# Attention's PSUM tiles: two banks for the scores of both maps, a head's output and norm together, one bank for transposes

## The chip, the cores and the metric

The kernel runs on one core of a Trainium2 chip. The metric is the device time of one execution in microseconds (us). Engines are named as in the profile: PE is the matmul engine (TensorE), PEld its weight loads, DVE VectorE, ACT ScalarE, POOL GpSimd, SP the engine that issues the transfers. PSUM is the memory that PE writes, and DVE and ACT read: eight banks, each of 128 partitions by 512 float32 here.

## What is computed

One layer of a bidirectional encoder, for 512 positions of 1024 channels in float32: a modulated RMS norm, three token mixers side by side (differential attention, HGRN2, GLA), their outputs merged through sigmoid gates, an output projection, then a squared-ReLU MLP and a last norm. The change touches differential attention alone, which has 4 heads. Each head has two maps of 64 query and key channels, and values of 128 channels:

```python
scores = jnp.einsum('bhiqd,bhikd->bhiqk', qb, k).astype(jnp.float32) * scale
scores = scores - slopes[:, None, None, None] * dist
p = jax.nn.softmax(scores, axis=-1)
w = p[:, :, 0] - lam * p[:, :, 1]
return jnp.einsum('bhqk,bhkv->bhqv', w.astype(v.dtype), v)
...
o = rms_norm(o, subln_g) * (1.0 - lam_init)
```

Positions are swept in query blocks of 128, so a head has four of them.

## The kernel before

A float32 product is made of three matmuls: each operand is split into a high part and a low part (suffixes h and l), and hi x hi, lo x hi and hi x lo are summed in one PSUM bank. All wide projections are made so, by `mm3` (L220 to L222): for a gate such as gb5 there are 8 slices of 128 input channels (h0 to h7) and so 24 matmuls of 512 columns. A weight is loaded raw, cast to its high part on ACT (L215) and subtracted to its low part on DVE (L216).

PSUM has three pools: `pm` with three banks (wide projections, gates, merges), `pl` with three (`ps_lv`) and `pt` with two (`ps_ms`). In attention, `pl` holds scores and `pt` the transposes, a head's output and the sum of its norm.

For each head and query tile, `attention(hd)` (L795 to L829) issues: six score matmuls, three for each of the two maps. Map 0 sits on partitions 0 to 63 and map 1 on 64 to 127, so each uses half of the array's rows (L807); a DVE operation for each map that adds the position penalty and takes the row maximum (L811), an exponential on ACT (L814), the sums' reciprocals and the weighted difference of the maps on DVE (L817 to L820), four transposes on PE (L823) and four copies on ACT (L825). After the four query tiles come the head's output `oa` (L828, four float32 matmuls) and `head_norm`: Square on ACT (L643), a matmul with ones that sums over partitions (L645), Ln and Exp on ACT (L177, L178, with a table load each), the scaling on DVE (L647, out An0sq to An3sq), and the split into An0oh and An0ol (L184, L185). These are inputs to `upa0` to `upa7` in the loop behind attention, next to the gates `ga0` to `ga7` (`proj_a`).

Between these pieces of attention the kernel has PE work that does not depend on it: a queue of generators (`pump`, `later`, `need`) holds the merge of the other two mixers, `merge_bc(m)`, with the gates `gb` and `gc` and the products `up`. `merge_bc` also loads modulation tiles of 512 KB (`ada16` to `ada47`, four of them for each m) and reduces each on DVE (`ada_tile`, L164). They share four buffers with the raw weights. The order of instructions on each engine is not that of the code: it is set when the kernel is built, by a scheduler that replays the program against its own model of durations and takes whichever instruction is ready; buffers of a pool bound what is ready. On the chip each engine runs its instructions strictly in that order, and an instruction waits by semaphore for the others that it needs.

Of the kernel before, what the change touches and what calls it, by code (L numbers as in the profile page):

```python
# [11 lines left out]
F32 = mybir.dt.float32  # L12
# [5 lines left out]
PSUM = bass.MemoryType.PSUM  # L18

P = 128  # L20
S = 512
# [33 lines left out]
def tile_trunk(ctx, tc, xT, cols, lam_p, w2blk, ada, slab, wtok, wlr, wck, wcq, wg, watt, wgate, wup_bc, wup_a, wout,  # L55
# [4 lines left out]
    def pool_of(name, n, side="left"):  # L60
        return tc.tile_pool(name=name, bufs=n, side=side, reuse_waits="tile")
# [15 lines left out]
    sm = ms_.enter_context(pool_of("sm", 4))  # L77
    sm.tile([P, 8], F32, tag="fill", name="smfill")
    pm = ctx.enter_context(tc.tile_pool(name="pm", bufs=3, space=PSUM))
    pl = ctx.enter_context(tc.tile_pool(name="pl", bufs=3, space=PSUM))  # L80

    def st(name, dt=F32, pool=None):
        return (pool or gp).tile([P, S], dt, tag="t", name=name)
# [4 lines left out]
    def ps_lv(name):  # L88
        return pl.tile([P, S], F32, tag="lv", name=name)

    def ps_ms(name):
        return pt.tile([P, S], F32, tag="ms", name=name)
# [21 lines left out]
    ones128 = c2.tile([P, P], F32, name="ones128")  # L114
# [60 lines left out]
    def rstd_of(ms, name, pool):  # L175
        L = st(name + "l", pool=pool)
        A.activation(L, ms, AF.Ln, bias=eps[:, 0:1])  # L177
        A.activation(L, L, AF.Exp, scale=-0.5)  # L178
        return L

    def split(src, name, pool):

        hi, lo = (pool.tile([P, S], F32R, tag="t", name=name + e) for e in "hl")
        A.copy(hi, src)  # L184
        V.tensor_tensor(lo, src, hi.bitcast(F32), ALU.subtract)  # L185
        return hi, lo
# [8 lines left out]
    def pump(n):  # L195

        while queue and n > 0:
            try:
                next(queue[0])
                n -= 1  # L200
            except StopIteration:
                queue.popleft()
# [67 lines left out]
    with tc.tile_pool(name="ad0", bufs=8, side="right", reuse_waits="tile") as ad0, \  # L270
# [59 lines left out]
        for k in range(KT):  # L330
# [12 lines left out]
            f = t  # L343
# [20 lines left out]
                for u in us:  # L364
                    mm3(slab_ps[u], wh[:, u * P:(u + 1) * P], wl[:, u * P:(u + 1) * P], hi, lo, False, k == KT - 1)
        lb, neglam, gsub, gb40, masks, bm, w2b, nd = small_operands()
    pt = ctx.enter_context(tc.tile_pool(name="pt", bufs=2, space=PSUM))

    def proj(src, name):
        wh, wl = weights(src, name, [P, KT, P])  # L370
# [267 lines left out]
                                  masks[:, li - 2, :].unsqueeze(1).to_broadcast([P, 8, 64]),  # L638
                                  ps.rearrange("p (n t) -> p n t", n=8))

    def head_norm(o, n, blk, g, extra, pool, dst):
        sq = st(n + "sq", pool=pool)
        A.activation(sq, o, AF.Square)  # L643
        ms = ps_ms(n + "ms")
        T.matmul(ms, blk, sq, start=True, stop=True)  # L645
        rs = rstd_of(ms, n + "rs", pool)
        V.scalar_tensor_tensor(sq, o, g, rs, ALU.mult, ALU.mult)  # L647
        if extra is not None:
            V.scalar_tensor_tensor(sq, sq, 0.5, extra, ALU.mult, ALU.mult)
        return split(sq, n + "o", dst)  # L650
# [69 lines left out]
    for j in range(2):  # L720
        npump = NP[j]
        def done(pr, o, j=j):
            if j == 0:
                need(f_bg[1])
                silu_of(0)
                silu_of(1)
            obc[j] = head_norm(o, f"Hn{j}", blk64, C("g_hg"), sg[j], cp[j], op)
        scan_tile(f"H{j}", cp[j], gp, gp, *hg[j], (0, 64), 0, (j,), f_bi, npump, done)
# [4 lines left out]
    def gdone(pr, o):  # L733
        need(f_gate)
        if pr == 0:
            tables_of_logs(last_tanh[0])
        obc[2 + pr] = head_norm(o, f"Gn{pr}", blk64, C("g_gl"), sg[2 + pr], cp[0], op)
# [46 lines left out]
    zs.close()  # L784
    ys.close()
    zs, ys = ExitStack(), ExitStack()
    oap = zs.enter_context(pool_of("oap", 8))
    fp = ys.enter_context(pool_of("fp", 8, "right"))
    es = ExitStack()
    ep = es.enter_context(pool_of("ep", 12, "right"))  # L790
    wtp = es.enter_context(pool_of("wtp", 4, "right"))
    part = []
    oa = []

    def attention(hd):  # L795
        slope = 2.0 ** (-2 * (hd + 1))
        qh, ql, kh, kl = qk[hd]
        wT = [st(f"wT{hd}{k}", pool=wtp) for k in range(4)]
        for qt in range(4):
            qs = slice(qt * P, (qt + 1) * P)  # L800
            e = []
            mx = sm.tile([P, 8], F32, tag="mx", name=f"mx{hd}{qt}")
            sc = [ps_lv(f"s{hd}{qt}{i}") for i in range(2)]
            for n_, (q_, k_) in enumerate(((qh, kh), (qh, kl), (ql, kh))):
                for i in range(2):
                    rr = slice(64 * i, 64 * i + 64)
                    T.matmul(sc[i], q_[rr, qs], k_[rr, :], start=n_ == 0, stop=n_ == 2)  # L807
            pump(NA)
            for i in range(2):
                s_ = st(f"e{hd}{qt}{i}", pool=ep)  # L810
                V.tensor_tensor_reduce(s_, sc[i], nd[:, 384 - P * qt:896 - P * qt], scale=slope, scalar=-3e38,  # L811
                                       op0=ALU.add, op1=ALU.max, accum_out=mx[:, i:i + 1])
                V.tensor_scalar(mx[:, 2 + i:3 + i], mx[:, i:i + 1], -1.0, None, ALU.mult)  # L813
                A.activation(s_, s_, AF.Exp, bias=mx[:, 2 + i:3 + i], accum_out=mx[:, 4 + i:5 + i])  # L814
                e.append(s_)
            pump(NA)
            V.reciprocal(mx[:, 6:8], mx[:, 4:6])  # L817
            V.tensor_tensor(mx[:, 7:8], mx[:, 7:8], neglam, ALU.mult)
            V.tensor_scalar(e[0], e[0], mx[:, 6:7], None, ALU.mult)  # L819
            V.scalar_tensor_tensor(e[0], e[1], mx[:, 7:8], e[0], ALU.mult, ALU.add)  # L820
            ps = ps_ms(f"wt{hd}{qt}")
            for k in range(4):
                T.transpose(ps[:, k * P:(k + 1) * P], e[0][:, k * P:(k + 1) * P], ident)  # L823
            for k in range(4):
                A.copy(wT[k][:, qs], ps[:, k * P:(k + 1) * P])  # L825
        o = ps_ms(f"oa{hd}")
        for k in range(4):
            T.matmul(o, av[k][:, hd * P:(hd + 1) * P], wT[k], start=k == 0, stop=k == 3)  # L828
        oa.append(head_norm(o, f"An{hd}", ones128, gsub, None, ep, oap))  # L829


    def merge_bc(m):
# [32 lines left out]
    for hd in range(4):  # L865
        need(f_att[hd])
        attention(hd)
# [19 lines left out]
    zs.close()  # L887
    ys.close()
    ms_.close()

    gtm = lambda m: modc[:, 16 + m:17 + m]
    amlp = const.tile([P, 8], F32, name="amlp")
# [304 lines left out]
    with tc.manual_schedule(engines=ENGINES):  # L1197
# [227 lines left out]
        for u in range(4, 16):  # L1425
            g, i = divmod(u, 4)
# [161 lines left out]
```

## Time and profile before

| | us |
|---|---|
| median of 3 runs | 867.02 |
| lowest and highest | 863.91, 867.43 |
| the profiled execution, own time | 867.18 |
| its span, first to last instruction | 865.4 |
| PE busy | 848.5 |
| DVE busy | 600.5 |
| ACT busy | 432.4 |

The span is what the rows of the trace cover; the execution's own time is 1.8 us longer. Attention's first score starts at 234.4 us and the last head's output ends at about 418 us of the span. A busy PE is one with a matmul under way; matmuls overlap by their pipeline, so a matmul's duration (0.39 us for 512 columns) is longer than the step from its start to the next one's, and the steps are what adds up to time.

### The profile page before, as it was taken

The numbers are of one execution on the slowest core, as the hardware profiler recorded it, in microseconds if no ns is written. First come the engines' busy times: TensorE is split into PE (matmuls) and PEld (weight loads), VectorE is DVE, ScalarE is ACT, GpSimd is POOL, SyncE is SP. The second block draws the span as 40 slices with busy tenths as digits, with TensorE's granted clock in tenths as the row PEclk, the third lists the DMA queues.
The fourth block names the chain that finished last, engine by engine and source line by source line (L and its number), as shares of the span: only waits on it lengthen the run. The fifth ranks groups of instructions, "written<-read, shape, count | busy, mean of one in ns | idle before, by whom it ended". The sixth has DMA issues, their size and how long they took to land.

```text
span 865.4 us, 14018 instructions
## 1 busy us (share of the span) xinstructions
PE 848.5 (98%) x5638; PEld 718.3 (83%) x5638; DVE 600.5 (69%) x1055; ACT 432.4 (50%) x788; POOL 26.4 (3%) x26
## 2 busy tenths in 40 slices
PE   7999999999999999999999999999999999999995
PEld 4797878888777777777788899999999999999885
DVE  8788889586687686866166658766666666766445
ACT  5686877454363554546345436834443443444423
POOL 3800000000000000000000000000000000000000
PEclk9999999999999999999999999999999999999998
DMA  9943120112546454644134502332322333333202
GB/s 337 402 134 100 50 74 27 50 39 75 185 131 195 146 174 143 221 169 122 61 98 147 181 15 60 112 98 98 98 98 98 98 98 108 110 106 116 76 23 98
DMA packets 32816, 103.15 MB, mean 119 GB/s; under 512 B 3664, under 2 KB 6128, under 8 KB 32752
## 3 DMA queue, kind: packets, MB, share of 16 engines
q1 hardware_dynamic: 32752, 102.26, 35.6%
q8 instruction: 44, 0.72, 0.4%
q14 instruction: 20, 0.16, 0.1%
HBM read 100.15 MB, written 2.10 MB: 118 GB/s over the span
## 4 chain that ended last, share of the span: by engine, by line
PE 88%; DVE 5%; ACT 3%; DMA 2%; issue 1%; SPq 0%; DVEq 0%; POOLq 0%; ACTq 0%
PE w L222 7%; PE w L220 7%; PE w L221 7%; PE s L807 2%; PE sl L361 2%; PE ou L221 2%; PE ou L220 2%; PE ou L222 2%; PE oa L828 2%; PE tp L388 1%; PE tp L389 1%; PE tp L387 1%; DMA wsl3r<-slab 1%; PE up L220 1%; PE wt L823 1%; DMA ada<-ada 1%
## 5 line engine op out<-in xcount | busy, mean ns | idle before, releaser
L164 DVE CUSTOM_DVE_ANT_0 ada<-ada,cb,col 128x1024 f32<-128x1024 f32 x32 | 41.1, 1283 | 33.6 <-DMA ada<-ada 33.6
L1168 DVE SCALAR_TENSOR_TENSOR x<-w,modc,x 128x512 f32<-128x512 f32 (+1 forms) x35 | 24.6, 704 | 32.7 <-PE w L222 32.7
L814 ACT ACTIVATE e<-e,mx 128x512 f32<-128x512 f32 x32 | 22.9, 719 | 21.0 <-DVE mx L813 21.0
L164 DVE CUSTOM_DVE_ANT_0 ada<-ada,cps,col 128x1024 f32<-128x1024 f32 x16 | 19.9, 1274 | 2.2 <-ACT cb L355 2.2
L811 DVE CUSTOM_DVE_ANT_0 e<-s,nd 128x512 f32<-128x512 f32 x32 | 20.8, 686 | 0.0
L825 ACT COPY wT<-wt 128x128 f32<-128x128 f32 x64 | 12.3, 280 | 14.5 <-PE wt L823 14.5
L1131 DVE SCALAR_TENSOR_TENSOR r<-r 128x512 f32<-128x512 f32 x24 | 16.6, 690 | 0.4
L926 DVE SCALAR_TENSOR_TENSOR x<-ou,modc,x 128x256 f32<-128x256 f32 (+1 forms) x12 | 6.8, 570 | 10.9 <-PE ou L222 10.9
L828 PE MATMUL oa<-wT,av 128*128 128x512 f32 x32 | 14.4, 592 | 0.0
L820 DVE SCALAR_TENSOR_TENSOR e<-e,mx,e 128x512 f32<-128x512 f32 x16 | 12.0, 750 | 0.3
L937 ACT ACTIVATE q<-x 128x256 f32<-128x256 f32 (+1 forms) x11 | 5.2, 470 | 13.1 <-DVE x L926 13.1
L880 DVE SCALAR_TENSOR_TENSOR gas<-gas,upa 128x512 f32<-128x512 f32 x8 | 5.4, 686 | 8.8 <-PE upa L222 8.8
L1177 ACT ACTIVATE q<-x 128x256 f32<-128x256 f32 (+1 forms) x9 | 4.6, 514 | 13.4 <-DVE x L1168 13.4
L828 PEld LDWEIGHTS oa<-wT,av 128*128 128x128 f32 x32 | 6.0, 189 | 6.1 <-issue 5.5
L823 PEld LDWEIGHTS wt<-ident,e 128*128 128x128 f32 x64 | 7.6, 140 | 3.0 <-issue 0.7
L310 POOL TENSOR_TENSOR hf<-x,rx 128x512 f32<-128x512 f32 x7 | 10.0, 1429 | 0.0
L823 PE MATMUL wt<-ident,e 128*128 128x128 f32 x64 | 9.8, 275 | 0.0
L647 DVE SCALAR_TENSOR_TENSOR Hn1sq<-H1o,col,Hn1rsl 128x512 f32<-128x512 f32 x1 | 0.8, 751 | 12.8 <-ACT Hn1rsl L178 12.8
L341 ACT ACTIVATE hf<-hf,modc,amix 128x512 f32<-128x512 f32 x7 | 5.7, 816 | 5.8 <-DVE modc L164 5.7
L883 ACT ACTIVATE mgh<-part 128x512 fp32r<-128x512 f32 x8 | 5.0, 632 | 7.2 <-DVE part L881 7.2
L647 DVE SCALAR_TENSOR_TENSOR An3sq<-oa,gsub,An3rsl 128x512 f32<-128x512 f32 x1 | 0.8, 751 | 10.8 <-ACT An3rsl L178 10.8
L819 DVE TENSOR_SCALAR e<-e,mx 128x512 f32<-128x512 f32 x16 | 7.7, 481 | 0.0
(7151 smaller groups left out, 3306.3 us busy)
## 6 DMA issues: line engine op xcount, KB each, us to landing
ada<-ada SPq DMA_DIRECT2D x48, 512.0 KB, 4.4
x<-xT SPq DMA_DIRECT2D x16, 256.0 KB, 4.8
outT<-o SPq DMA_DIRECT2D x8, 256.0 KB, 2.2
w10r<-w SPq DMA_DIRECT2D x2, 512.0 KB, 6.2
w11r<-w SPq DMA_DIRECT2D x2, 512.0 KB, 5.1
w12r<-w SPq DMA_DIRECT2D x2, 512.0 KB, 3.2
w13r<-w SPq DMA_DIRECT2D x2, 512.0 KB, 3.8
w14r<-w SPq DMA_DIRECT2D x2, 512.0 KB, 3.1
```

What stands on the lines that cost most here:

```text
L164: V.tensor_tensor_reduce(w, w, c_, scale=1.0, scalar=C("ada_b", ADA_BLK[u]), op0=ALU.mult, op1=ALU.add, accum_out=o)
L220: T.matmul(ps, wh, xh, start=first, stop=False)
L221: T.matmul(ps, wh, xl, start=False, stop=False)
L222: T.matmul(ps, wl, xh, start=False, stop=last)
L361: T.matmul(slab_ps[u], w_[:, u * P:(u + 1) * P], x_, start=k == 0 and w_ is wh and x_ is hi, stop=False)
L807: T.matmul(sc[i], q_[rr, qs], k_[rr, :], start=n_ == 0, stop=n_ == 2)
L811: V.tensor_tensor_reduce(s_, sc[i], nd[:, 384 - P * qt:896 - P * qt], scale=slope, scalar=-3e38, op0=ALU.add, op1=ALU.max, accum_out=mx[:, ...
L814: A.activation(s_, s_, AF.Exp, bias=mx[:, 2 + i:3 + i], accum_out=mx[:, 4 + i:5 + i])
L823: T.transpose(ps[:, k * P:(k + 1) * P], e[0][:, k * P:(k + 1) * P], ident)
L828: T.matmul(o, av[k][:, hd * P:(hd + 1) * P], wT[k], start=k == 0, stop=k == 3)
L1131: V.scalar_tensor_tensor(self.r[j], self.r[j], 0.0, self.r[j], ALU.max, ALU.mult)
L1168: V.scalar_tensor_tensor(x, self.ps[:, sl], modc[:, 40 + self.m:41 + self.m], x, ALU.mult, ALU.add)
```

## The change

When the mixers have closed, the pools `pl` and `pt` are closed too (five banks). In their place come `pd`, two tiles of two banks each, and `pt1` with one bank. A score tile of `pd` holds both maps of one query tile, one in each bank. A head's output takes a tile of the same pool: the output in its first bank, the sum of its norm in the second. The one bank of `pt1` is for the transposes. Behind attention's loops `pd` and `pt1` are closed again and pools like the old ones are opened for the MLP.

```diff
--- before.py
+++ after.py
@@ -77,7 +77,8 @@
     sm = ms_.enter_context(pool_of("sm", 4))
     sm.tile([P, 8], F32, tag="fill", name="smfill")
     pm = ctx.enter_context(tc.tile_pool(name="pm", bufs=3, space=PSUM))
-    pl = ctx.enter_context(tc.tile_pool(name="pl", bufs=3, space=PSUM))
+    banks = ctx.enter_context(ExitStack())
+    pl = banks.enter_context(tc.tile_pool(name="pl", bufs=3, space=PSUM))
 
     def st(name, dt=F32, pool=None):
         return (pool or gp).tile([P, S], dt, tag="t", name=name)
@@ -364,7 +365,7 @@
                 for u in us:
                     mm3(slab_ps[u], wh[:, u * P:(u + 1) * P], wl[:, u * P:(u + 1) * P], hi, lo, False, k == KT - 1)
         lb, neglam, gsub, gb40, masks, bm, w2b, nd = small_operands()
-    pt = ctx.enter_context(tc.tile_pool(name="pt", bufs=2, space=PSUM))
+    pt = banks.enter_context(tc.tile_pool(name="pt", bufs=2, space=PSUM))
 
     def proj(src, name):
         wh, wl = weights(src, name, [P, KT, P])
@@ -638,10 +639,11 @@
                                   masks[:, li - 2, :].unsqueeze(1).to_broadcast([P, 8, 64]),
                                   ps.rearrange("p (n t) -> p n t", n=8))
 
-    def head_norm(o, n, blk, g, extra, pool, dst):
+    def head_norm(o, n, blk, g, extra, pool, dst, ms=None):
         sq = st(n + "sq", pool=pool)
         A.activation(sq, o, AF.Square)
-        ms = ps_ms(n + "ms")
+        if ms is None:
+            ms = ps_ms(n + "ms")
         T.matmul(ms, blk, sq, start=True, stop=True)
         rs = rstd_of(ms, n + "rs", pool)
         V.scalar_tensor_tensor(sq, o, g, rs, ALU.mult, ALU.mult)
@@ -784,6 +786,11 @@
     zs.close()
     ys.close()
     zs, ys = ExitStack(), ExitStack()
+
+
+    banks.close()
+    pd = banks.enter_context(tc.tile_pool(name="pd", bufs=2, space=PSUM))
+    pt = banks.enter_context(tc.tile_pool(name="pt1", bufs=1, space=PSUM))
     oap = zs.enter_context(pool_of("oap", 8))
     fp = ys.enter_context(pool_of("fp", 8, "right"))
     es = ExitStack()
@@ -800,7 +807,8 @@
             qs = slice(qt * P, (qt + 1) * P)
             e = []
             mx = sm.tile([P, 8], F32, tag="mx", name=f"mx{hd}{qt}")
-            sc = [ps_lv(f"s{hd}{qt}{i}") for i in range(2)]
+            both = pd.tile([P, 2, S], F32, tag="s", name=f"s{hd}{qt}")
+            sc = [both[:, i, :] for i in range(2)]
             for n_, (q_, k_) in enumerate(((qh, kh), (qh, kl), (ql, kh))):
                 for i in range(2):
                     rr = slice(64 * i, 64 * i + 64)
@@ -823,10 +831,11 @@
                 T.transpose(ps[:, k * P:(k + 1) * P], e[0][:, k * P:(k + 1) * P], ident)
             for k in range(4):
                 A.copy(wT[k][:, qs], ps[:, k * P:(k + 1) * P])
-        o = ps_ms(f"oa{hd}")
+        both = pd.tile([P, 2, S], F32, tag="s", name=f"oa{hd}")
+        o, ms = both[:, 0, :], both[:, 1, :]
         for k in range(4):
             T.matmul(o, av[k][:, hd * P:(hd + 1) * P], wT[k], start=k == 0, stop=k == 3)
-        oa.append(head_norm(o, f"An{hd}", ones128, gsub, None, ep, oap))
+        oa.append(head_norm(o, f"An{hd}", ones128, gsub, None, ep, oap, ms))
 
 
     def merge_bc(m):
@@ -887,6 +896,9 @@
     zs.close()
     ys.close()
     ms_.close()
+    banks.close()
+    pl = banks.enter_context(tc.tile_pool(name="pl2", bufs=3, space=PSUM))
+    pt = banks.enter_context(tc.tile_pool(name="pt2", bufs=2, space=PSUM))
 
     gtm = lambda m: modc[:, 16 + m:17 + m]
     amlp = const.tile([P, 8], F32, name="amlp")
```

The same instructions remain on every engine, but their order moves. Three places follow. Names carry their tile's number: s20 is the score tile of head 2, query tile 0 (before, s200 and s201 are its two maps), e200 and e201 what DVE makes of its two maps, oa1 is the output of head 1; `x2` is two rows that read alike. In the order of after, line numbers behind the diff's lines are one to twelve higher.

PE, scores of head 2 in the order of before, between the merge up4 and the gate gb5: one map of query tile 1 and both of query tile 2, map by map.

```order
L222 MATMUL up42_3588<-Gn1oh_2672,ubc4l_3569 128x512
L807 MATMUL s211_3545<-k2h_3000,qh2_2943 128x512
L807 MATMUL s211_3545<-k2l_3001,qh2_2943 128x512
L807 MATMUL s211_3545<-k2h_3000,ql2_2944 128x512
L807 MATMUL s220_3643<-k2h_3000,qh2_2943 128x512
L807 MATMUL s220_3643<-k2l_3001,qh2_2943 128x512
L807 MATMUL s220_3643<-k2h_3000,ql2_2944 128x512
L807 MATMUL s221_3644<-k2h_3000,qh2_2943 128x512
L807 MATMUL s221_3644<-k2l_3001,qh2_2943 128x512
L807 MATMUL s221_3644<-k2h_3000,ql2_2944 128x512
L220 MATMUL gb5p_3616<-h0h_260,gb5h_3612 128x512
```

PE, the same head in the order of after, between up5 and gb6:

```order
L223 MATMUL up52_3736<-Gn1oh_2672,ubc5l_3725 128x512
L815 MATMUL s21_3541<-k2h_3004,qh2_2948 128x512 x2
L815 MATMUL s21_3541<-k2l_3005,qh2_2948 128x512 x2
L815 MATMUL s21_3541<-k2h_3004,ql2_2949 128x512 x2
L815 MATMUL s22_3639<-k2h_3004,qh2_2948 128x512 x2
L815 MATMUL s22_3639<-k2l_3005,qh2_2948 128x512 x2
L815 MATMUL s22_3639<-k2h_3004,ql2_2949 128x512 x2
L221 MATMUL gb6p_3764<-h0h_260,gb6h_3760 128x512
```

Both maps of a query tile now alternate, and query tiles 1 and 2 stand in one block; head 2 has moved from ahead of gb5 to behind up5. Its first query tile, s20, stands 40 matmuls earlier, right behind oa1.

DVE in the order of before, around the scaling of head 1's norm (An1sq): the reads of head 2's scores stand in banks of their own.

```order
L811 ISA e200_3495,mx20_3457<-s200_3458,nd_563 128x512
L811 ISA mx20_3457 128x1
L811 ISA e201_3499,mx20_3457<-s201_3459,nd_563 128x512
L811 ISA mx20_3457 128x1
L811 ISA e210_3579,mx21_3543<-s210_3544,nd_563 128x512
L811 ISA mx21_3543 128x1
L164 ISA ada39_3761,modc_158<-ada39_3761,cb_157,col_129 128x1024
L164 ISA modc_158 128x1
L813 TENSOR_SCALAR mx20_3457<-mx20_3457 128x1 x2
L647 SCALAR_TENSOR_TENSOR An1sq_3441<-oa1_3436,gsub_551,An1rsl_3445 128x512
L813 TENSOR_SCALAR mx21_3543<-mx21_3543 128x1
```

DVE in the order of after, the same place:

```order
L217 TENSOR_TENSOR gb6l_3761<-gb6r_3758,gb6h_3760 128x1024
L165 ISA ada42_3932,modc_158<-ada42_3932,cb_157,col_129 128x1024
L165 ISA modc_158 128x1
L819 ISA e200_3492,mx20_3455<-s20_3456,nd_563 128x512
L819 ISA mx20_3455 128x1
L819 ISA e201_3496,mx20_3455<-s20_3456,nd_563 128x512
L819 ISA mx20_3455 128x1
L821 TENSOR_SCALAR mx20_3455<-mx20_3455 128x1
L165 ISA ada43_3935,modc_158<-ada43_3935,cb_157,col_129 128x1024
L165 ISA modc_158 128x1
L649 SCALAR_TENSOR_TENSOR An1sq_3440<-oa1_3435,gsub_551,An1rsl_3443 128x512
L821 TENSOR_SCALAR mx20_3455<-mx20_3455 128x1
```

The reads of s20 and the scaling of An1sq now have ada42 and ada43 ahead of them (and ada40 and ada41 four and two rows further up), where before there was ada39.

PE in the order of before, around the sum of the last head's norm (An3ms), which stands 22 matmuls behind that head's output oa3:

```order
L222 MATMUL ga3p_4282<-h3h_375,ga3l_4279 128x512
L220 MATMUL ga3p_4282<-h4h_414,ga3h_4278 128x512
L645 MATMUL An3ms_4201<-An3sq_4199,ones128_116 128x512
L221 MATMUL ga3p_4282<-h4l_415,ga3h_4278 128x512
L222 MATMUL ga3p_4282<-h4h_414,ga3l_4279 128x512
L220 MATMUL ga3p_4282<-h5h_446,ga3h_4278 128x512
```

PE in the order of after, the same place, from two matmuls behind oa3 down to the first use of An3oh (the sum's tile is oa3's own):

```order
L223 MATMUL ga4p_4328<-h7h_510,ga4l_4325 128x512
L647 MATMUL oa3_4183<-An3sq_4188,ones128_116 128x512
L221 MATMUL upa2_4361<-An0oh_3072,ua2h_4357 128x512
L222 MATMUL upa2_4361<-An0ol_3073,ua2h_4357 128x512
L223 MATMUL upa2_4361<-An0oh_3072,ua2l_4358 128x512
L221 MATMUL upa2_4361<-An1oh_3447,ua2h_4357 128x512
L222 MATMUL upa2_4361<-An1ol_3448,ua2h_4357 128x512
L223 MATMUL upa2_4361<-An1oh_3447,ua2l_4358 128x512
L221 MATMUL upa2_4361<-An2oh_3822,ua2h_4357 128x512
L222 MATMUL upa2_4361<-An2ol_3823,ua2h_4357 128x512
L223 MATMUL upa2_4361<-An2oh_3822,ua2l_4358 128x512
L221 MATMUL upa0_4245<-An3oh_4195,ua0h_4241 128x512
```

In the order of before, 9 matmuls of upa0, 13 of ga3, the norm's sum, 11 of ga3 and 9 of upa1 stand between oa3 and the first use of An3oh. Here it is three of ga4, the norm's sum and nine of upa2; on ACT the cast of ua2 and the tanh of ga4 have come in between Square and Ln.

## Rows read from the trace of the kernel before

**Rows 1.** The page, busy time of each engine (part 1) and the chain of waits (part 4).
```profile
PE 848.5 (98%) x5638; PEld 718.3 (83%) x5638; DVE 600.5 (69%) x1055; ACT 432.4 (50%) x788; POOL 26.4 (3%) x26
...
PE 88%; DVE 5%; ACT 3%; DMA 2%; issue 1%; SPq 0%; DVEq 0%; POOLq 0%; ACTq 0%
```

**Rows 2.** Windows: stretch, length, busy (x instructions) of PE, PEld, DVE, ACT, POOL, clock, DMA, GB/s.
```profile
120.00:125.00 5.00, 4.36 (x17) 3.93 (x18) 4.97 (x8) 4.94 (x11) 0.00 (x0) 0.66 0.53 157
300.00:350.00 50.00, 50.00 (x216) 37.26 (x216) 37.72 (x89) 24.59 (x59) 0.00 (x0) 1.00 0.46 150
```

**Rows 3.** Timeline of PE, the last head's output and norm.
```profile
414.94 3.59 PE L828 MATMUL oa<-wT,av 128*128 128x512 f32 x8
...
418.60 0.40 PE L221 MATMUL upa<-An0ol,ua0h 128*128 128x512 f32 x1
...
423.15 0.40 PE L220 MATMUL ga3p<-h4h,ga3h 128*128 128x512 f32 x1
423.38 1.02 PE L645 MATMUL An3ms<-An3sq,ones 128*128 128x512 f32 x2
...
424.48 0.40 PE L222 MATMUL ga3p<-h4h,ga3l 128*128 128x512 f32 x1
...
428.82 0.39 PE L220 MATMUL upa<-An3oh,ua0h 128*128 128x512 f32 x1
```

**Rows 4.** Timeline of PE, a three-matmul score block: start, duration, operation.
```profile
332.87 0.39 PE L222 MATMUL gc4p<-h3h,gc4l 128*128 128x512 f32 x1
...
334.08 0.50 PE L220 MATMUL gc4p<-h4h,gc4h 128*128 128x512 f32 x1
```

**Rows 5.** Timeline of PE, a block of six.
```profile
353.93 0.39 PE L222 MATMUL gc5p<-h7h,gc5l 128*128 128x512 f32 x1
354.25 0.50 PE L807 MATMUL s<-k2h,qh 64*128 64x512 f32 x2
...
355.14 0.50 PE L220 MATMUL up<-Hn0oh,ubc5h 128*128 128x512 f32 x1
```

**Rows 6.** Timeline of PE, a block of nine.
```profile
340.31 0.39 PE L222 MATMUL up<-Gn1oh,ubc4l 128*128 128x512 f32 x1
...
342.21 0.50 PE L220 MATMUL gb5p<-h0h,gb5h 128*128 128x512 f32 x1
```

**Rows 7.** Timeline of DVE around the second head's norm; in brackets the idle before.
```profile
325.89 1.28 DVE L164 CUSTOM_DVE_ANT_0 ada<-ada,cb,col 128x1024 f32<-128x1024 f32 x1 [3.26 <-DMA ada<-ada]
...
330.83 1.28 DVE L164 CUSTOM_DVE_ANT_0 ada<-ada,cb,col 128x1024 f32<-128x1024 f32 x1 [3.64 <-DMA ada<-ada]
...
335.81 1.28 DVE L164 CUSTOM_DVE_ANT_0 ada<-ada,cb,col 128x1024 f32<-128x1024 f32 x1 [2.55 <-DMA ada<-ada]
...
337.22 0.68 DVE L811 CUSTOM_DVE_ANT_0 e<-s,nd 128x512 f32<-128x512 f32 x1
...
339.05 1.28 DVE L164 CUSTOM_DVE_ANT_0 ada<-ada,cb,col 128x1024 f32<-128x1024 f32 x1
...
340.38 0.74 DVE L647 SCALAR_TENSOR_TENSOR An1sq<-oa,gsub,An1rsl 128x512 f32<-128x512 f32 x1
```

**Rows 8.** Timeline of ACT, the last head's norm.
```profile
418.57 0.60 ACT L643 ACTIVATE An3sq<-oa 128x512 f32<-128x512 f32 x1 [2.50 <-PE oa L828]
419.19 1.28 ACT L177 ACT_TABLE_LOAD   x1
424.44 0.69 ACT L177 ACTIVATE An3rsl<-An3ms,eps 128x512 f32<-128x512 f32 x1 [3.97 <-PE An3ms L645]
...
426.44 0.63 ACT L178 ACTIVATE An3rsl<-An3rsl 128x512 f32<-128x512 f32 x1
...
427.92 0.62 ACT L184 CAST An3oh<-An3sq 128x512 fp32r<-128x512 f32 x1
```

**Rows 9.** Timeline of PE where its clock fell.
```profile
118.70 0.38 PE L387 MATMUL tp<-wt20h,h0h 128*128 128x256 f32 x1 [0.55 <-ACT wt20h L215]
120.64 1.65 PE L588 MATMUL H0kv<-val,H0kT 128*128 128x128 f32 x6 [1.55 <-ACT H0kT L583]
```

## The prediction

> **What bounds the kernel now.** I read the page first. Its part 1 gives PE 98% of the span and its chain of waits gives PE 88% [rows 1], so PE is the engine that sets the end; an edit pays only if it makes PE's own work shorter, and costs whatever it makes PE wait. Then I read the windows: around attention PE is busy in all 50.00 us of the stretch 300 to 350, at a granted clock of 1.00 [rows 2]. Nothing else than PE has to be priced, except where one of the other engines comes late for PE.
>
> Two things about PE in that stretch. An ordinary 512-column matmul follows the last after 0.227 us (418.60 to 423.15 is twenty steps) [rows 3]. A score matmul uses half of the array's rows (K is 64), and going from full rows to half and back costs extra. A block of three score matmuls of one map lasts from 332.87 to 334.08 between the starts of its neighbours, 1.21 us, less one ordinary step 0.98 [rows 4]. A block of six, both maps in turn, lasts from 353.93 to 355.14, again 0.98 net [rows 5]: its matmuls start in pairs (each row there is x2), so the second map is free. A block of nine, one pair block and one single-map block behind it, lasts from 340.31 to 342.21, 1.67 net [rows 6]. So a pass of three steps costs 0.69 and the opening of a block 0.29.
>
> **The change part by part.** The scores of both maps now share a tile of two banks, so each q tile asks for its six matmuls together. In PE's order of before the 96 score matmuls stand in six blocks of six, seven of three, four of nine, and one of three that transposes cut in two: 22 passes and 19 openings, 22 x 0.69 + 19 x 0.29 = 20.7 us. In the order of after they are six blocks of six and five of twelve: 16 passes, 11 openings, 11.0 + 3.2 = 14.2 us. Gain 6.5 us. All other matmuls are the same in number and kind, so this is the whole of the gain on PE.
>
> Head 0's scores come later, because the two-bank tiles exist only when the mixers' last PSUM tile (the norm of the last GLA pair) has been read: they stand behind almost all of gate gc1 instead of ahead of up00. PE has gate matmuls to do there, so I cost the move at nothing; if that cover failed it would be a wait of at most a few us. One bank for the transposes instead of two: each group of four is read by four short copies and groups stand tens of matmuls apart; nothing.
>
> What costs is the ring of two tiles. A head takes, in order, its last score tile, the tile of its output (with the norm's sum in the second bank), the next head's first scores, and then the next head's second scores need the first of these tiles back. In the new PE order s20 (head 2, q tile 0) comes right behind oa1, and s21 needs the tile of s20 after both DVE reads of it (L811 of before), and s22 the tile of oa1 after the norm's last DVE operation (L647). In DVE's order those reads stand behind ada40, ada41, ada42, and the norm's operation behind ada43. Those are the modulation operations that wait for their 512 KB loads: 325.89, 330.83, 335.81, an idle of 3.26 and 3.64 ahead of each, about 4.95 apart [rows 7]; only the last came faster (339.05), which is 4.4 apart over the three. Before, the scores of head 2 had banks of their own and PE did not ask DVE for anything here.
>
> The wait: from oa1's start PE has the four matmuls of the output (in the trace oa3, 414.94 to 418.60 less a step, 3.43), the block s20 (0.98), three of gb5, 24 of gc5 and 12 of up5, 39 x 0.227 = 8.85, and the norm's matmul, 423.15 to 424.48 less two steps, 0.87 [rows 3]: PE stands at s21 14.1 us after oa1's start. DVE: ada39 stands between the merges of up4, whose matmuls end some 5 us before oa1 starts, so it can end between 5 us before and 3 us after; then three loads x 4.95, and two reads of 0.68 [rows 7]: 11.2 to 19.2 after oa1's start, middle 16.2. So PE waits 0 to 5.1 us; the upper half is likelier since the loads in front of ada39 go at the same pace, and I take 3.1. Queued behind s21 are s22 and gate gb6, and nothing else can use PE. s22 waits for ada43 and the norm's operation, 1.28 + 0.74 [rows 7], less the block s21, 0.92: 1.1 us (0 to 2). Gate gb7 then needs the bank of gc6, whose tanh on ACT stands behind the exponentials of s23 and these behind DVE's late softmax: 0 to 2.5, I take 1.2. s11 and s31 need the same tiles, but there DVE's order has no load between the head's output and these reads; nothing.
>
> The tail. Before, the last head's norm was covered: oa3 at 414.94, then 9 of upa0, 13 of ga3, the norm's sum, 11 of ga3, 9 of upa1, and An3oh is wanted at 428.82 [rows 3]. In the new order oa3 is followed by three of ga4, the norm's sum, nine of upa2, and then An3oh. By the rows: Square starts 3.63 after oa3's start and takes 0.60 [rows 8]; PE is there at 4.11, so the sum waits 0.15 and is readable 1.06 later (424.44 less 423.38) [rows 3, 8], at 5.3. ACT has in between the cast of ua2 and the tanh of ga4, about 0.6 each like the other 512-column ones, which ends at 5.45 and starts upa2 there (a wait of 0.3); then table load 1.28, Ln 0.69, a table load again, Exp 0.63 and, behind DVE's 0.74 [rows 7], the cast 0.62 [rows 8]: An3oh at 10.7. PE is through with upa2 at 7.5 and waits 3.2. Behind it ga5's weights are still being split on ACT and DVE after that chain: 0 to 1.5, I take 0.6. Tail: 0.15 + 0.3 + 3.2 + 0.6 = 4.2 us (3.0 to 5.5).
>
> The clock. It fell once, to the half level (1.2 GHz): 0.66 on average over 120 to 125, after PE idles of 0.55 (118.70) and 1.55 us (120.64) [rows 2, 9]: 0.34 of 5 us missing is 3.4 us at half rate, in which 1.7 us of PE's work is lost, a little less where PE had none. The waits at s21 and s22 are together longer than those two, so I take one such loss of 1.5 (0 to 4, if it also falls in the tail).
>
> The Trainium skill speaks to this too: its page "TensorE: Matmul & The Clock Gate", section "A second HAM failure mode: psum-queue depth-cycling", says that cycling through PSUM banks makes PE idle for short moments between groups, often enough that its clock goes back and forth between half and full rate. The stretch 300 to 350 cycles through banks and shows 1.00, against that sentence; the change makes the ring shorter, which is the case it describes, and a clock that went back and forth there would be the fourth rival below. The page "TensorEngine Tiling (Array Packing)", section "Gotcha 1: PSUM Pressure", says that row tiles write to different banks and so raise the pressure on PSUM; no row of before shows PE waiting for that, and it is the s21 term that would.
>
> **Sum.** Against the profiled execution's own 867.18 us (span 865.4 and 1.8 around it; the median of the three runs is 867.02): -6.5 + 3.1 + 1.1 + 1.2 + 4.2 + 1.5 = +4.6, 871.8 us.
>
> **The rivals.**
> First, the clock stays up: 870.3. For it: the one fall of before came where PE had been idle twice within 2 us. Against: the wait at s21 is longer than both of those together.
> Second, on the other side, the loads come in time: if ada39 ends 3 us or more before oa1's start, the reads of s20 are done before PE reaches s21, and s22 and gb7 wait for nothing. The tail remains: 867.2 - 6.5 + 4.2 = 864.9, with a tail at its lower bound 863.7. For it: DVE is only 69% busy and one load came in 3.2 us. Against: each of the other loads had an idle in front of it.
> Third, the change doesn't do what it says: with both maps in one tile PE runs them one after the other, 32 passes in 11 blocks, 22.1 + 3.2 = 25.3 instead of 14.2, 882.9; or at only half of that, 877. Against: the pair block of before wrote two banks just so.
> Fourth, the clock falls in two or three places and the waits are at their upper ends: 867.2 - 6.5 + 5.1 + 2 + 2.5 + 5.5 + 4 = 879.8; half of the excess over the forecast gives 875.8.
>
> **How the numbers follow.** What one can tell from no change here is 0.5%, 4.3 us: faster is under 862.7, slower over 871.4. Chances: forecast with one fall 0.45 (own range 869.5 to 874), clock stays up 0.18, loads in time 0.17, no pairing 0.04, upper ends 0.16. Slower: 0.6 of the forecast's 0.45, 0.2 of the first rival's, all of the last two: 0.27 + 0.04 + 0.04 + 0.16 = 0.51. Faster: 0.4 of the second rival's 0.17, where tail and ring both come cheap: 0.07. The rest, 0.42, is no change. The range leaves out half of the second rival's share below 865 and about 0.1 above 876.5.
>
> **What would show it.** Right: s rows in the profile of after all x2; PE idles with a DVE releaser ahead of s21 and s22 and with ACT ahead of upa0 after oa3, of 3 us each or so; DVE idle on ada loads ahead of the reads of s20; PE busy down by some 6 us. Wrong: PE idle under 5 us in all between 230 and 460, or score steps that are no longer x2, or waits at s02, s11 or s31.

## The result and the profile after

The change makes the kernel slower by about 0.65%. In its own comparison it took 871.65 us in the median (870.05 to 873.05, five times) against 866.07 before (863.91 to 867.43), ratio 1.0065 with a 95% interval of 1.0049 to 1.0081; timed again beside the experiments it came to 871.51 us, ratio 1.0066 (1.0049 to 1.0083). The forecast was 871.8.

The profiled execution took 870.05 us (span 868.3), the shortest of the five. Its page, the rows that answer to [rows 1]:

```profile
PE 844.7 (97%) x5638; PEld 715.5 (82%) x5638; DVE 599.3 (69%) x1055; ACT 433.1 (50%) x788; POOL 26.4 (3%) x26
...
PE 81%; DVE 8%; DMA 5%; ACT 4%; issue 2%; SPq 0%; DVEq 0%; POOLq 0%; ACTq 0%
```

PE is busy 3.8 us less than before, yet the span is 2.9 us longer: PE has lost seven points of the chain, and DVE, the transfers and ACT have gained them. What PE waited for between 225 and 475, where before there was no such wait (columns: engine, line waited at, what it waited for, us in total, times, longest):

```profile
PE s L815 <- DVE mx L819: 3.4, 1, 3.4
PE upa L221 <- ACT An3oh L185: 3.0, 1, 3.0
PE ga6p L221 <- DVE gas L889: 0.5, 1, 0.5
PE ga5p L223 <- DVE ga5l L217: 0.3, 1, 0.3
PE s L815 <- DVE mx L821: 0.3, 1, 0.3
```

And the windows, with the columns of [rows 2]:

```profile
120.00:125.00 5.00, 4.11 (x23) 3.56 (x24) 4.97 (x8) 4.94 (x11) 0.00 (x0) 1.00 0.57 136
300.00:330.00 30.00, 30.00 (x147) 24.06 (x147) 24.62 (x55) 15.40 (x40) 0.00 (x0) 1.00 0.55 168
345.00:360.00 15.00, 11.30 (x41) 7.91 (x40) 12.63 (x28) 4.71 (x10) 0.00 (x0) 0.77 0.63 190
```

PE is full at 1.00 in a stretch without a wait (300 to 330). In 345 to 360 it idles 3.7 us, and its clock, 0.77 on average, was at the half level (1.2 GHz) for 0.23 x 15 / 0.5 = 6.9 us. In 120 to 125, where before it fell, it did not fall this time.

The difference between the two profiles comes from three stretches. All of attention and the loop behind it lie between the first matmul of gate gb0 and the first of the output projection (`ou`), and PE runs the same matmuls there in both; first before, then after:

```profile
214.25 0.39 PE L220 MATMUL gb0p<-h0h,gb0h 128*128 128x512 f32 x1
...
468.53 0.39 PE L220 MATMUL ou<-mgh,wo0h 128*128 128x512 f32 x1
```

```profile
213.11 0.39 PE L221 MATMUL gb0p<-h0h,gb0h 128*128 128x512 f32 x1
...
472.51 0.39 PE L221 MATMUL ou<-mgh,wo0h 128*128 128x512 f32 x1
```

That is 254.3 us before and 259.4 after: attention costs 5.1 us more. The profiles differ by 2.9 only, because the change came to gb0 1.1 us earlier (no fall of the clock at 120) and went through a part of the MLP 1.1 us faster (last section).

The gain is there. PE's timeline around a block of twelve, against [rows 4 to 6]:

```profile
250.94 0.39 PE L223 MATMUL up<-Hn1oh,ubc1l 128*128 128x512 f32 x1
251.25 0.50 PE L815 MATMUL s<-k0h,qh 64*128 64x512 f32 x2
...
252.52 0.39 PE L815 MATMUL s<-k0h,ql 64*128 64x512 f32 x2
252.84 0.50 PE L221 MATMUL up<-Gn0oh,ubc1h 128*128 128x512 f32 x1
```

Twelve matmuls for what nine cost: 1.90 us between the neighbours' starts, 1.67 net, all in pairs.

The place at s21, on DVE (against [rows 7]; start, duration, operation, in brackets the idle before):

```profile
332.68 1.28 DVE L165 CUSTOM_DVE_ANT_0 ada<-ada,cb,col 128x1024 f32<-128x1024 f32 x1
...
339.48 1.28 DVE L165 CUSTOM_DVE_ANT_0 ada<-ada,cb,col 128x1024 f32<-128x1024 f32 x1 [3.64 <-DMA ada<-ada]
...
344.38 1.29 DVE L165 CUSTOM_DVE_ANT_0 ada<-ada,cb,col 128x1024 f32<-128x1024 f32 x1 [3.61 <-DMA ada<-ada]
...
349.18 1.28 DVE L165 CUSTOM_DVE_ANT_0 ada<-ada,cb,col 128x1024 f32<-128x1024 f32 x1 [2.37 <-DMA ada<-ada]
...
350.39 0.68 DVE L819 CUSTOM_DVE_ANT_0 e<-s,nd 128x512 f32<-128x512 f32 x1
...
352.88 0.74 DVE L649 SCALAR_TENSOR_TENSOR An1sq<-oa,gsub,An1rsl 128x512 f32<-128x512 f32 x1
```

and on PE, from head 1's output to the middle of gb6:

```profile
333.86 3.59 PE L837 MATMUL oa<-wT,av 128*128 128x512 f32 x8
...
351.75 0.80 PE L815 MATMUL s<-k2h,qh 64*128 64x512 f32 x2 [3.42 <-DVE mx L819]
...
353.68 0.80 PE L815 MATMUL s<-k2h,qh 64*128 64x512 f32 x2 [0.28 <-DVE mx L821]
...
357.99 0.62 PE L221 MATMUL gb6p<-h2h,gb6h 128*128 128x512 f32 x1
358.41 0.43 PE L222 MATMUL gb6p<-h2l,gb6h 128*128 128x512 f32 x1
...
358.92 0.40 PE L221 MATMUL gb6p<-h3h,gb6h 128*128 128x512 f32 x1
```

The first row of DVE is ada39; ada40, 41 and 42 follow, each behind an idle for its transfer. DVE reads s20 at 350.39, 16.5 us after oa1's start, and PE starts s21 as the second read ends. From there its steps are 0.42 us (357.99 to 358.41) instead of 0.227, until 358.4.

The tail on PE and then on ACT, against [rows 3] and [rows 8]:

```profile
428.00 3.59 PE L837 MATMUL oa<-wT,av 128*128 128x512 f32 x8
...
438.66 0.50 PE L221 MATMUL upa<-An3oh,ua0h 128*128 128x512 f32 x1 [3.04 <-ACT An3oh L185]
...
442.78 0.47 PE L221 MATMUL ga6p<-h0h,ga6h 128*128 128x512 f32 x1 [0.48 <-DVE gas L889]
...
444.16 0.40 PE L221 MATMUL ga5p<-h1h,ga5h 128*128 128x512 f32 x1
```

```profile
431.63 0.60 ACT L644 ACTIVATE An3sq<-oa 128x512 f32<-128x512 f32 x1 [7.46 <-PE oa L837]
432.13 0.61 ACT L216 CAST ua2h<-ua2r 128x512 fp32r<-128x512 f32 x1
432.63 0.60 ACT L412 ACTIVATE gas<-ga4p 128x512 f32<-128x512 f32 x1
433.25 1.28 ACT L178 ACT_TABLE_LOAD   x1
434.55 0.69 ACT L178 ACTIVATE An3rsl<-oa,eps 128x512 f32<-128x512 f32 x1
...
437.99 0.62 ACT L185 CAST An3oh<-An3sq 128x512 fp32r<-128x512 f32 x1 [0.82 <-DVE An3sq L649]
```

An3oh is used 10.66 us after oa3's start; the prediction had it ready at 10.7 and PE waiting 3.2. From oa3 to the last row PE takes 16.16 us. By the prediction's own prices its work there (the output 3.43, the norm's sum 0.87, 28 ordinary matmuls of 0.227) is 10.7 us, so the tail costs 5.5.

### The profile page after: what moved, and what is told of

The parts are those of the page before. It is cut to its first block, busy times and chain, and to the rows that moved or that the text cites. A ratio compares the mean times of both kernels' runs of the same rounds, so it can differ in the third digit from the quotient of the medians.

```text
span 868.3 us, 14019 instructions
## 1 busy us (share of the span) xinstructions
PE 844.7 (97%) x5638; PEld 715.5 (82%) x5638; DVE 599.3 (69%) x1055; ACT 433.1 (50%) x788; POOL 26.4 (3%) x26
## 4 chain that ended last, share of the span: by engine, by line
PE 81%; DVE 8%; DMA 5%; ACT 4%; issue 2%; SPq 0%; DVEq 0%; POOLq 0%; ACTq 0%
PE w L222 7%; PE w L223 7%; PE w L221 7%; DMA ada<-ada 3%; PE sl L362 2%; PE ou L222 2%; PE ou L223 2%; PE ou L221 2%; PE tp L389 1%; PE oa L837 1%; PE tp L390 1%; PE tp L388 1%; PE s L815 1%; DMA wsl3r<-slab 1%; DVE ada L165 1%
## 5 line engine op out<-in xcount | busy, mean ns | idle before, releaser
L1143 DVE SCALAR_TENSOR_TENSOR r<-r 128x512 f32<-128x512 f32 x24 | 16.5, 688 | 0.4
L949 ACT ACTIVATE q<-x 128x256 f32<-128x256 f32 (+1 forms) x11 | 5.2, 470 | 13.2 <-DVE x L938 13.2
L542 ACT ACTIVATE Gea<-Gea 128x512 f32<-128x512 f32 x7 | 4.4, 631 | 6.2 <-PE Gl4h L628 4.7
```

Source lines behind the costliest of these rows:

```text
L1143: V.scalar_tensor_tensor(self.r[j], self.r[j], 0.0, self.r[j], ALU.max, ALU.mult)
```

## The experiments

The runs were timed in two groups, e1 to e4 and e5 to e8, each beside the kernel before: 867.15 us in the first group, 865.50 in the second. So ratios are compared, not times across the groups. In the edits, LA is the number of gates ga that are queued ahead of the attention loops, and m the number of a merge.

| run | edit | us | ratio to before, 95% interval |
|---|---|---|---|
| e1_tail | after + four gates ahead | 865.78 | 0.9985 (0.9974 to 0.9997) |
| e2_loads | after + two loads moved | 867.17 | 1.0002 (0.9991 to 1.0013) |
| e3_both | after + both | 861.92 | 0.9941 (0.9928 to 0.9955) |
| e4_both_on_before | before + both | 866.52 | 1.0002 (0.9990 to 1.0015) |
| e5_after_again | after | 871.51 | 1.0066 (1.0049 to 1.0083) |
| e6_one_bank_tiles | after, four tiles of one bank | 872.53 | 1.0086 (1.0070 to 1.0102) |
| e7_one_load | after + one load moved | 869.54 | 1.0053 (1.0038 to 1.0069) |
| e8_three_both | after + four gates ahead, three loads moved | 858.70 | 0.9926 (0.9909 to 0.9942) |

**The tail.** e1_tail's edit:

```diff
-LA = 2
+LA = 4
```

> The changed kernel with four instead of two of the gates ga queued ahead of the attention loops, so that PE has gate matmuls left behind the last head's output. Theory (the tail waits add up to 4.5 us of the changed kernel's time and nothing else there is hidden): PE's waits after the last output go (An3oh 3.0, ga6 0.5, ga5l 0.3 and the two small ones), the wait of 3.4 us at s21 with its fall of the clock stays, and the time is 871.65 - 4.5 = 867.1 us (866 to 868.5), ratio to before 1.001. Rival (the tail's chain only moves: the loop behind attention is bound by the same casts and tanh, so PE waits there later): 870 to 872.

Measured 865.78 us, 0.8% under the change. The waits of that run between 225 and 475, all of them:

```profile
PE s L815 <- DVE mx L819: 3.5, 1, 3.5
PE s L815 <- DVE mx L821: 0.9, 1, 0.9
```

Every wait of the tail is gone and the one at s21 is still there, so the two are separate, and the loop behind attention takes the time back nowhere. The ratio fell by 0.8% or 6.9 us, where 4.5 were expected. The intervals on the two ratios (0.12 and 0.16%) leave that figure open by some 1.7 us either way, so the 5.5 us that the tail costs by PE's steps lie inside it, and a further cause isn't shown. The profiled execution of this run was the slowest of its twelve: it came to gb0 2.9 us later than the profile of the change, with a clock of 0.83 over 120 to 130.

**The loads.** e2_loads:

```diff
-        for u in range(16 + 4 * m, 20 + 4 * m):
+        for u in range(16 + 4 * m, (18 if m == 5 else 20) + 4 * m):
             ada_tile(u, ada_load(u), cb)
+        if m == 7:
+            for u in (38, 39):
+                ada_tile(u, ada_load(u), cb)
```

> The changed kernel with two of the modulation loads of merge 5 (ada38, ada39) moved behind those of merge 7, LA as it was. Theory (s21 waits because DVE's reads of s20 stand behind loads that land 5 us apart, and the clock's fall there comes from that wait): no PE wait of over 1 us at s21, granted clock 1.00 through 345 to 360, and 3.4 + 0.3 + 3.1 = 6.8 us less: 864.9 us (863.5 to 866.5). Rival A (the ring of two tiles itself makes PE wait, whatever stands ahead of the reads): the wait stays, 871. Rival B (the wait goes, but the clock falls there for another reason): 868.

Measured 867.17 us. Its waits and its window:

```profile
PE upa L221 <- ACT An3oh L185: 3.1, 1, 3.1
PE ga6p L221 <- DVE gas L892: 0.5, 1, 0.5
PE ga5p L223 <- DVE ga5l L217: 0.3, 1, 0.3
PE gb7p L221 <- ACT gcs L412: 0.2, 1, 0.2
```

```profile
345.00:360.00 15.00, 14.90 (x70) 10.69 (x69) 12.53 (x32) 6.74 (x12) 0.00 (x0) 1.00 0.61 191
```

No wait at s21, clock 1.00: both of the theory's signs, and both rivals fall. The time is 0.64% under the change, 5.5 us, again open by some 1.7; 6.8 was expected. In the profiles the stretch from oa1's start to gb6's matmul of h3h, with the same matmuls in both, takes 18.52 us against 25.05 in the change (333.86 to 358.92), 6.5 less.

**Both, and both without the change.** e3_both and e4_both_on_before make the two edits together, once on the changed kernel and once on the kernel before.

> Both edits together. Theory (the two waits are independent, and what is left is the gain of the score blocks): 871.65 - 4.5 - 6.8 = 860.4 us (859 to 862), ratio 0.993; PE waits for nothing over 1 us between 230 and 470. Rival (what one wait gives back the other takes): 864 to 867.

> The same two edits on the kernel before, with its single-bank tiles. Theory (before had neither wait, so there is nothing to win): within 0.2% of 866.5, so that the difference to the run with both edits on the changed kernel is the score blocks' gain alone, about 6 us. Rival (the two edits are worth something by themselves): 861 to 864, and the score blocks are worth less than 3 us.

Measured 0.9941 and 1.0002. The two edits give the kernel before nothing within 0.15%, since it had neither wait (its profile with them has one of 1.3 us at a transpose, 0.15% of the time, which is as much as the interval can hide); on the changed kernel they give 1.2%. So what is left in e3_both is the score blocks' gain, 0.6% or 5.2 us, with one wait still in it, and it is the wait at s22:

```profile
PE s L815 <- DVE An1sq L649: 1.0, 1, 1.0
...
```

The only other wait there is the 0.2 us at gate gb7.

**The change again.**

> The changed kernel once more, unedited, beside the others of this job, since its first five times and those of the edits come from different jobs. Theory: 871 to 873 us, PE waits of 3.4 us at s21 and 3.0 us at An3oh again, and the clock falls after the first. Rival (the first comparison was a lucky or unlucky day): within 0.3% of before.

Measured 871.51 us. Two rows of its windows:

```profile
345.00:360.00 15.00, 10.38 (x38) 7.19 (x37) 12.42 (x28) 4.05 (x9) 0.00 (x0) 0.77 0.57 182
430.00:450.00 20.00, 16.97 (x60) 11.66 (x59) 10.88 (x16) 11.35 (x16) 0.00 (x0) 0.91 0.21 66
```

PE waits 4.3 us at s21, 0.3 at s22 and 3.0 at An3oh. The fall at s21 comes again, and in this run there is a second in the tail: 0.09 x 20 / 0.5 = 3.6 us at half rate, which the first profile doesn't have. It cost almost nothing: from oa3's start to the same matmul of ga5 it is 16.28 us here and 16.16 there, and the waits of 0.5 and 0.3 at ga6 and ga5l are gone in exchange.

**One-bank tiles.** e6_one_bank_tiles:

```diff
-    pd = banks.enter_context(tc.tile_pool(name="pd", bufs=2, space=PSUM))
+    pd = banks.enter_context(tc.tile_pool(name="pd", bufs=4, space=PSUM))
...
-            both = pd.tile([P, 2, S], F32, tag="s", name=f"s{hd}{qt}")
-            sc = [both[:, i, :] for i in range(2)]
+            sc = [pd.tile([P, S], F32, tag="s", name=f"s{hd}{qt}{i}") for i in range(2)]
...
-        both = pd.tile([P, 2, S], F32, tag="s", name=f"oa{hd}")
-        o, ms = both[:, 0, :], both[:, 1, :]
+        o, ms = (pd.tile([P, S], F32, tag="s", name=f"{n}{hd}") for n in ("oa", "om"))
```

> The changed kernel with the same four banks as four tiles of one bank instead of two tiles of two: each map's scores, a head's output and the sum of its norm take one each; the one bank for transposes stays. Theory (what makes PE wait at s21 is that a two-bank tile comes back only when both its halves have been read, so that no score can start early): no wait at s21 and no fall of the clock there, the tail's waits stay at 4 to 4.5 us, and the score blocks, which start singly again (21 passes and 16 openings by PE's order, 19.1 us), lose 4.9 us of the gain: 867.15 - 1.6 + 4.4 = 870 us (868.8 to 871.2). Rival A (the loss is in the four banks, however they are cut): a wait of 3 us at s21 stays, 874 or more. Rival B (the one bank for transposes is what costs): PE waits at wt tiles for the copies on ACT.

Measured 872.53 us, a ratio of 1.0086 where 1.003 was expected: a miss. Besides the 3.0 us at An3oh, PE waited here:

```profile
...
PE s L814 <- DVE mx L818: 1.6, 1, 1.6
```

The wait at head 2 is halved, not gone: one map can start early, the next needs a bank that DVE has not read yet. The clock falls behind it as before (0.50 in 353 to 356). So the size of the tile is not all that makes PE wait: cut singly, four banks are still too few under reads that come 8 us after the write (342.24 to 350.39 in this run). In PE's order of this run the scores stand in 16 blocks again instead of 11, so the tile of two banks is what buys the pairing. In the tail the clock fell here as well, to 0.83 over 430 to 450, which the expectation didn't have; the miss was not taken apart further. Rival B has nothing: no transposes waited.

**One load.** e7_one_load is e2_loads with ada39 alone moved.

> As the run with two loads moved, but only one (ada39), nothing else changed. Theory (each load in the chain is worth up to 5 us of DVE's lateness, and the chain was 3.4 us too long at s21): the wait at s21 falls to 0 to 0.8 us, the one behind it at s22 is about 1.2, no fall of the clock, 868.2 us (867 to 869.5). Rival (the fall of the clock comes with any wait there): the clock under 0.9 in 345 to 360 and 870 us.

Measured 869.54 us, ratio 1.0053 where 1.001 was expected: a miss as well, on the side of the rival. Its waits at scores, and its window:

```profile
...
PE s L815 <- DVE mx L821: 2.2, 1, 2.2
PE s L815 <- DVE An1sq L649: 1.0, 1, 1.0
...
```

```profile
345.00:360.00 15.00, 11.74 (x43) 8.43 (x42) 12.92 (x32) 4.54 (x9) 0.00 (x0) 0.77 0.57 188
```

The load before the gap was not worth 5 us. Measured from oa1's start, DVE's first read of s20 came after 16.5 us in the change (333.86 to 350.39), after 15.3 with one load moved and 12.1 with two (e2_loads). With four gates ahead it came after 16.6 us with no load moved (e1_tail), 13.2 with two (e3_both) and 11.1 with three (e8_three_both, next). So the first load is worth 1.2 us, two are worth 3.4 to 4.4, three 5.5. And the clock fell here after waits of 2.2 and 1.0 us, but not in e3_both after 1.0 alone.

**Three loads.** e8_three_both takes e3_both one load further (ada37 to ada39 behind merge 7).

> Four gates ahead, as in the run on the tail, and three loads of merge 5 moved instead of two. Theory: the last wait of 1.0 us at s22, which the run with both edits still had, goes, and with it that microsecond: 860.9 us (859.5 to 862.2), no PE wait over 0.5 us between 230 and 470. Rival (it comes back as waits of gate gb7 or of the merges, whose loads are now later): 862 or more.

Measured 858.70 us, ratio 0.9926 (0.9909 to 0.9942), the fastest kernel here; as a ratio 0.993 was expected. In its profile the list of PE's waits between 225 and 475 is empty, and

```profile
230.00:470.00 240.00, 240.00 (x1082) 184.75 (x1082) 163.05 (x328) 120.78 (x242) 0.00 (x0) 1.00 0.47 151
```

PE is full through all of attention, as it was before. 865.5 less 858.7 is 6.8 us, and the profile has the same in the stretch from gb0 to `ou`, 247.6 us against 254.3:

```profile
212.81 0.39 PE L221 MATMUL gb0p<-h0h,gb0h 128*128 128x512 f32 x1
...
460.42 0.39 PE L221 MATMUL ou<-mgh,wo0h 128*128 128x512 f32 x1
```

This is the score blocks' gain with no wait against it. One of the blocks of six is cut in two by transposes in this run's order, which the change's own order doesn't have.

## Why the prediction was right

The terms and their causes were the right ones; that the time was met to 0.2 us is in part luck. The sum started from 867.18 us, and the five runs of before beside the change have a median of 866.07: the difference was forecast as +4.6 and measured as +5.6. And errors cancel among the terms. By PE's steps in the profiles, attention costs 5.1 us more, of which the tail is +5.5 and the place at s21 +6.9 (oa1's start to gb6's matmul of h3h, 25.05 us, against 18.16 for the same matmuls in e8_three_both); that leaves -7.3 for the score blocks. The sum had +4.2, +6.9 (s21, s22, gb7 and the clock together) and -6.5.

- *Score blocks, -6.5 us:* right, and a little small. e8_three_both, the change without its waits, is 6.8 us under before, and by e4_both_on_before the same kind of edits (two loads moved there, not three) gave before nothing. One thing was missed: behind a head's output the block s20 costs less, 4.20 us from oa1's start to the next ordinary matmul less a step (337.39 is its first, 338.29 the end) against 3.43 + 0.98 in the sum. Three blocks stand so, 0.6 us.
- *s21, 3.1 us (0 to 5.1):* 3.4, and the mechanism is the one named: reads behind ada40 to ada42, by DVE's rows and by e2_loads, where two loads less take it to zero. That the size came out is in part luck, for the reads came later than the sum had them and PE a little later too. The middle of 11.2 and 19.2 is 15.2 and not the 16.2 of the prediction; 16.2 is the case in which ada39 ends at oa1's start, and so it did (333.96 against 333.86). From there ada40 came 6.8 us after ada39's start instead of 4.95, so that the reads ended 17.8 us after oa1's start, close to what the 3.1 us imply.
- *s22, 1.1 us:* 0.3. The block s21 in front of it ran at half clock and used the time up; in e3_both, at full clock, it is 1.0. The size was right for full clock.
- *gb7, 1.2 us (0 to 2.5):* nothing in the change. The term was mis-sized: PE came there later than the sum had it, after the half clock, and that may be why ACT was in time; in e2_loads, with no half clock, it is 0.2.
- *The tail, 4.2 us (3.0 to 5.5):* 3.04 + 0.48 + 0.34 shown as waits, and some 1.6 in longer steps that the trace does not mark as idle: 5.5 by steps, the upper bound. Right in its steps from the Square (431.63, 3.63 after oa3's start) to An3oh (10.66); what was too small is the time around the norm's sum and behind An3oh, at ga5 and ga6. That it is the tail is shown by e1_tail, which took all of its waits away.
- *The clock, 1.5 us (0 to 4):* one fall at s21, as forecast, but it cost more: 6.9 us at half rate, less 0.3 of idle in it, are 3.3 us of PE's work. In the profile pair it was offset by the fall at 120 that before had and after had not.

The runs of one kernel differ by 3 us. Their granted clocks go with it, 0.993 in the shortest run of the change (870.05 us) and 0.987 in the longest (873.05), so more falls of the clock in the longer runs are the likely reason; where those falls lie was seen in the profiled executions alone. The change's two profiles differ by 1.3 us: -0.6 ahead of gb0, +0.8 in attention, nearly all of it at s21, and +1.1 in the MLP, where the clock is 1.00 in both.

Of the signs, the pairs, the two waits and DVE's idle on the loads came as written, and PE idled 7.6 us between 230 and 470. PE's busy time fell by 3.8 us and not by some 6; work at the half level counts in it at its longer time.

Of the rivals, the first (the clock stays up) fell with the 0.77 at s21 in both profiles. Loads in time is what e2_loads made true by hand, and it came to 867.17, level with before, where 2.3 us under it was forecast, with the tail still there. The third is refuted by the x2 rows of the block of twelve. The fourth's clock fell in two places in one of two profiles of the change, but the waits at s21, s22 and gb7 were not at their upper ends; the tail, by steps, was. The Trainium skill's sentence on cycling through PSUM banks (page "TensorE: Matmul & The Clock Gate", section "A second HAM failure mode: psum-queue depth-cycling") is not borne out as far as the cycling goes: e8_three_both cycles through the same two tiles, has no PE wait there, and shows a clock of 1.00 over 240 us. In attention and the loop behind it the clock fell only behind a PE wait, though not behind every one (last section).

## What to carry to other kernels

A ring of large PSUM tiles ties the engine that fills it to the slowest reader in it, so before asking what the larger tile saves, look at what stands ahead of its readers in the order of their own engine; here it was a chain of loads that nobody else needed soon. Moving three of those loads, and keeping work behind the last head, turned a change of +0.7% into one of -0.7%. And price a wait of PE with what its clock may lose behind it: at s21 that was about as much again, in the tail nothing to 1.3 us.

## What the runs showed of the hardware

Behind the scores, after a PE wait of 3.4 us (4.3 in e5_after_again), of 1.6, and of 2.2 and 1.0 together, the clock fell to its half level and stayed there for 6 to 7 us (351.75 to 358.4 in the change); after a wait of 1.0 alone in e3_both it did not fall. The length of a wait does not settle it. The wait of 3.0 us at An3oh is in five profiles: the clock over 430 to 450 stayed at 1.00 in the change, e2_loads and e7_one_load, and was 0.91 in e5_after_again and 0.83 in e6_one_bank_tiles. What it cost there, from oa3's start to the same matmul of ga5, was 0.1 us (16.28) and 1.3 us (17.47) against 16.16. The same two idles at 118.95 and 120.89 (0.55 and 1.55 us, as in [rows 9]) left it at 1.00 in the profile of the change and took it to 0.66 before:

```profile
118.95 0.39 PE L388 MATMUL tp<-wt20h,h0h 128*128 128x256 f32 x1 [0.55 <-ACT wt20h L216]
120.89 0.60 PE L589 MATMUL H0kv<-val,H0kT 128*128 128x128 f32 x3 [1.55 <-ACT H0kT L584]
```

Near 186 us, among small matmuls, one idle of about 0.55 us stands in all ten profiles; behind it the clock was 0.89 over 180 to 196 in e2_loads and 1.00 in e3_both.

In the MLP, PE's steps between 533 and 558 were 0.113 us in some executions (543.52 to 544.20 is six, in the first profile of the change) and 0.118 in others (539.88 to 540.47 is five, before), 1.1 us over the stretch; the two profiles of the changed kernel differ so, 90.28 and 91.38 us from the first matmul `ou` to the first `w`, with the same instructions, and the profile of before has 91.37. The granted clock over 533 to 558 is 1.00 in all three. What sets it stays open.
